# First layer of a two-layer transformer: the token mixer re-ordered, attention values in plain float32

## The chip, the core and the metric

The kernel is one program on one core of a Trainium2 chip. The metric is its time on the device in microseconds (us). A profile of one execution shows the engines of the core: PE (matrix products), PEld (its weight loads), DVE and ACT (element-wise work), POOL and SP (here mostly issuing transfers).

## The reference, cut to what matters

The program computes a first layer (adaptive modulation, a mixer made of windowed attention and a gated convolution, then 16 experts) and a second network of feed-forward blocks and attention. Only the first layer's mixer is touched; `x` has 512 tokens of 1024 channels, `ctx` has 256:

```python
mod = silu(c) @ w_ada + b_ada            # six vectors of 1024; also for c_ctx
hc = modulate(rmsnorm(ctx, g_mix), csh1, csc1)
k_c, v_c = split(hc @ w_in[:, 512:768])
h = modulate(rmsnorm(x, g_mix), sh1, sc1)
q, k, v, bg, cg, hv = split(h @ w_in)    # 512, 128, 128, 512, 512, 512
att = windowed_attention(rope(q), rope(k), v, k_c, v_c, sink)
conv = bg * conv3(cg * hv)
x = x + gt1 * (concatenate([att, conv]) @ w_out)
```

Attention has 8 query heads in two key groups of four heads (group 0 and 1, 64 channels each). A block of 128 queries sees all 256 context keys and the 256 or 384 keys near it.

## The kernel before, in words

Most products are made in three parts (`mm3`, L247 to L249): both operands are split into a high and a low half in the type fp32r (`whi`, `wlo` for weights, by ACT in L161 and DVE in L162), and high x high, low x high and high x low are added up in PSUM. Weights come through a queue object, `W`: chunks of up to 1 MB are loaded by SP into a ring of four buffers, a unit of a chunk is split two units ahead of its use, and a chunk's buffer is free again when it has been split (or, for the raw `w_ada` chunks, multiplied). The order of the chunks is the order of the `plan_...` calls.

The mixer runs in these steps, which follow each other in the program:

- The first third of `w_ada` (8 chunks of 1 MB), multiplied as plain float32 with 32 columns of the array for each of four column groups (L478). While it loads, the six blocks of 128 token rows arrive; ACT and POOL find their norms and DVE scales them.
- Keys and values: for each of the six token blocks PE turns the rows (L294), ACT and DVE apply scale and shift to eight pieces of 128x128 each from PSUM and split the result (L519, L522, L523: `hcT`, `hT`), and 24 products of 256 columns make keys and values (in pA).
- Rotation and turning of the keys (L580), then 96 products of 512 columns for the queries, whose rotation and turning (L605) runs beside the convolution's products: 4 channel blocks x 3 projections x 24 products of 512 columns, in pB and pC by turns.
- Attention: for the eight pairs of query block and key group, `scores` (L687 to L703: products, maximum, exponential, scaling) is called one pair ahead of `values`. There PE turns the probabilities of four heads for one key block (L712, four turns of 128x128 into pB), ACT and DVE split them (`PTh`, `PTl`), and one `mm3` with `Vh`, `Vl` adds to pC; 36 such key blocks in all. `ada_group`, the second and the third part of `w_ada`, runs whole before the second and the fifth pair.
- The output projection: 8 x 4 x 2 `mm3` with `w_out`; when a block of 128 tokens is complete, DVE multiplies it (L786) and adds it to `X`, which POOL has loaded again from `x` (L733).

A scheduler places the instructions on each engine's queue; each engine works its queue off in order. PSUM has two buffers each of pA (two banks), pB and pC.

Of the kernel before, what the change touches and what calls it, by code (L numbers as in the profile page):

```python
# [9 lines left out]
F32 = mybir.dt.float32  # L10
# [180 lines left out]
def tile_net(ctx, tc, I, out):  # L191
# [149 lines left out]
    for c2 in range(2):  # L341
        cs = [W.chunk([(0, P, rows(w_in, 0, K, b0 + c2 * 256, 256))], (P, K, 256)) for b0 in (1280, 1792, 768)]
        for cc in range(2):
            for c in cs:
                W.unit(c, lambda v, cc=cc: v[:, :, cc * P:(cc + 1) * P])
    plan_ada(1)
    plan_ada(2)
# [102 lines left out]
    Vh = mixp.tile([P, 6, P], F32R, name="Vh")  # L450
    Vl = mixp.tile([P, 6, P], F32R, name="Vl")
# [6 lines left out]

    def token_rows(src, t):
        r = early.tile([P, D], F32, name="xrow", tag="xrow", bufs=6)  # L460
        nc.scalar.dma_start(out=r, in_=src[t * P:(t + 1) * P])
        return r
# [4 lines left out]
    def ada_rows(pool, g):  # L467


        bb = pool.tile([P, 512], F32, name="bb", tag="rp1", bufs=1)  # L470
# [3 lines left out]
        p = psB()  # L474
        for k in range(K):
            w = W.next()
            for j in range(4):
                PE.matmul(p[32 * j:32 * j + 32], cb[:, k].rearrange("p s c -> p (s c)"), w[:, j],  # L478
                          start=k == 0, stop=k == K - 1)
        V.tensor_add(bb, p, bb)  # L480
        return bb
# [12 lines left out]
    for r in rows_in:  # L494
        V.tensor_scalar(r, r, row_rstd(early, r, D), None, op0=OP.mult)
    m = ada_rows(early, 0)
# [16 lines left out]
    def modulated_into(pool, dst, t, sc, sh, pick=None):  # L513

        def put(g, m, pv):
            for a in range(m):
                k = g + a
                c_ = slice(t * P, (t + 1) * P)
                A.activation(dst[0][:, k, c_], pv[:, a], AF.Identity, scale=sc[:, k:k + 1], bias=sh[:, k:k + 1])  # L519
            tmp = pool.tile([P, 4, P], F32, name="mtmp", tag="mtmp", bufs=1)  # L520
            for a in range(m):
                V.tensor_scalar(tmp[:, a], pv[:, a], sc[:, g + a:g + a + 1], sh[:, g + a:g + a + 1], op0=OP.mult, op1=OP.add)  # L522
            V.tensor_sub(dst[1][:, g:g + m, c_], tmp, f(dst[0][:, g:g + m, c_]))  # L523
        return put

    hcT = qT.rearrange("p h s -> p (h s)").rearrange("p (s k n) -> p s k n", s=2, k=K)
    hcT = [hcT[:, 0], hcT[:, 1]]
    hT = pair("hT")
# [20 lines left out]
    def turned(b):  # L549
        xs, t, s = (hcT, b, 1) if b < TC else (hT, b - TC, 0)  # L550
        transposed(rows_in[b], K, modulated_into(early, xs, t, sc1[:, s], sh1[:, s]))
        return xs, t

    nxt = turned(0)
    for b in range(6):
        xs, t = nxt
        if b < 5:
            nxt = turned(b + 1)
        o = psA()[:, 0:256]
        for k in range(K):  # L560
            mm3(o, [x[:, k, t * P:(t + 1) * P] for x in xs], [x[:, k % 4] for x in ws[k // 4]], k == 0, k == K - 1)
        A.copy(out=kvs[:, b], in_=o)
    split(Vh, Vl, kvs[:, :, P:256])
    for b0 in (0, 2, 4):
# [11 lines left out]
        for s in range(2):  # L576
            p = psBC()
# [7 lines left out]

    a0, a1 = psA(), psA()
    qp = [a0[:, 0:512], a0[:, 512:1024], a1[:, 0:512], a1[:, 512:1024]]
    for u in range(4):
        w = W.next()
        for kk in range(2):  # L590
            k = u * 2 + kk
            for t in range(T):
                mm3(qp[t], [x[:, k, t * P:(t + 1) * P] for x in hT], [x[:, kk] for x in w], k == 0, k == K - 1)
    qks = []
    for t in range(T):
        qr = rope1(qp[t].rearrange("p (o h d) -> p o h d", o=1, d=HD), 1, H, t, early)
# [4 lines left out]
        for g in range(2):  # L601
            p = psA()
            pv = p[:, :512].rearrange("p (h t) -> p h t", h=4)
# [5 lines left out]
    for cblk in range(4):  # L609
        p3 = []  # L610
        for _ in range(3):
            p3.append(psBC())
            w = W.next()
            for k in range(K):
                mm3(p3[-1], [x[:, k] for x in w], [x[:, k] for x in hT], k == 0, k == K - 1)
        cg = early.tile([P, S], F32, name="cg", tag="rp1", bufs=1)
        A.copy(out=cg, in_=p3[0])
        u_ = early.tile([P, S + 2], F32, name="convu", tag="convu", bufs=1)
        V.memset(u_[:, 0:1], 0.0)
        V.memset(u_[:, S + 1:S + 2], 0.0)  # L620
        V.tensor_mul(u_[:, 1:S + 1], p3[1], cg)
        y = early.tile([P, S], F32, name="convy", tag="rp2", bufs=1)
        V.tensor_scalar(y, u_[:, 0:S], cw[:, cblk, 0:1], None, op0=OP.mult)
        V.scalar_tensor_tensor(y, u_[:, 1:S + 1], cw[:, cblk, 1:2], y, op0=OP.mult, op1=OP.add)
        V.scalar_tensor_tensor(y, u_[:, 2:S + 2], cw[:, cblk, 2:3], y, op0=OP.mult, op1=OP.add)
        V.tensor_mul(conv[:, cblk], p3[2], y)
# [5 lines left out]
    mixT = pair("mixT")  # L632
    for cblk in range(4):
        split(mixT[0][:, 4 + cblk], mixT[1][:, 4 + cblk], conv[:, cblk])
# [9 lines left out]
    def ada_group(g):  # L644
        m = ada_rows(att, g)
# [59 lines left out]

    def values(n, g, Pt, lo, hi):
        o = psC()
        blks = [0, 1] + list(range(2 + lo, 2 + hi))
        for z, blk in enumerate(blks):
# [6 lines left out]
        r = slice(g * 64, g * 64 + 64)  # L716
        ov = o[r].rearrange("p (i t) -> p i t", i=4)
        split(mixT[0][r, 0:4, n * P:(n + 1) * P], mixT[1][r, 0:4, n * P:(n + 1) * P], ov)

    todo = [(n, g) for n in range(T) for g in range(KV)]  # L720
    nxt = scores(*todo[0])
    for z, (n, g) in enumerate(todo):
# [56 lines left out]
    for t in range(T):  # L779
# [3 lines left out]
        for dh in range(2):  # L783
            tmp = att.tile([P, 512], F32, name="tmp", tag=("PTh", "PTl")[dh], bufs=2)
# [678 lines left out]
```

## Time and profile before

| what | us |
|---|---|
| median of three runs (2702.54 to 2704.97) | 2703.97 |
| the profiled execution's own time | 2703.63 |
| its span, first to last instruction | 2701.6 |
| PE busy in the span | 2568.8 |
| last product of the first `w_ada` part begins | 39.05 |
| first product of the convolution begins | 101.83 |
| last product of the convolution begins | 172.44 |
| first finished block of the output projection (L786) | 332.06 |
| first product of the experts (L905) | 388.91 |

Times inside the program count from the start of the span. The profiled execution lies within the runs' range, 0.34 us under their median, so differences worked out in it stand for the runs too.

### The profile page before, as it was taken

The numbers are of one execution on the slowest core, as the hardware profiler recorded it, in microseconds if no ns is written. First come the engines' busy times: TensorE is split into PE (matmuls) and PEld (weight loads), VectorE is DVE, ScalarE is ACT, GpSimd is POOL, SyncE is SP. The second block draws the span as 40 slices with busy tenths as digits, with TensorE's granted clock in tenths as the row PEclk, the third lists the DMA queues.
The fourth block names the chain that finished last, engine by engine and source line by source line (L and its number), as shares of the span: only waits on it lengthen the run. The fifth ranks groups of instructions, "written<-read, shape, count | busy, mean of one in ns | idle before, by whom it ended". The sixth has DMA issues, their size and how long they took to land.

```text
span 2701.6 us, 29081 instructions
## 1 busy us (share of the span) xinstructions
PE 2568.8 (95%) x12042; PEld 1879.9 (70%) x12042; DVE 1066.7 (39%) x1661; ACT 748.4 (28%) x1288; POOL 88.5 (3%) x142
## 2 busy tenths in 40 slices
PE   5988979999998999999999999999999899999999
PEld 3864744333433888878877878887879777878887
DVE  4646441222223433335533334333334566533332
ACT  4324320000002322223322223322223655322221
POOL 1000020000000000000000000000001100000000
PEclk8989979999999999999999999999999999999999
DMA  8226249999998322323222322323232111122321
GB/s 301 67 86 221 71 164 419 414 418 418 416 417 342 124 94 90 105 86 102 74 94 90 106 86 86 108 80 102 78 101 73 63 57 63 63 94 78 108 83 59
DMA packets 179251, 411.89 MB, mean 152 GB/s; under 512 B 7364, under 2 KB 120544, under 8 KB 151472
## 3 DMA queue, kind: packets, MB, share of 16 engines
q1 hardware_dynamic: 176928, 403.73, 40.7%
q0 software_dynamic: 1184, 2.97, 0.4%
q10 hardware_dynamic: 1008, 3.34, 0.3%
q8 instruction: 94, 1.54, 0.2%
q14 instruction: 37, 0.30, 0.0%
HBM read 407.92 MB, written 2.10 MB: 152 GB/s over the span
## 4 chain that ended last, share of the span: by engine, by line
PE 58%; issue 30%; DVE 4%; ACT 3%; DMA 3%; POOL 1%; ACTq 0%; POOLq 0%; DVEq 0%; SPq 0%
PE pA L905 8%; PE pA L247 7%; PE pA L248 7%; PE pA L249 7%; PE pB L905 4%; PE pC L248 2%; PE pC L247 2%; PE pC L249 2%; PE pB L249 2%; PE pB L247 2%; PE pB L248 2%; DMA wraw<-in_w_ada_dram 1%; PE pC L879 1%; PE pC L952 1%; PE ms L1334 1%
## 5 line engine op out<-in xcount | busy, mean ns | idle before, releaser
L161 ACT CAST whi<-wraw 128x1024 fp32r<-128x1024 f32 (+2 forms) x334 | 336.2, 1011 | 1107.6 <-PE pA L248 686.3
L162 DVE TENSOR_TENSOR wlo<-wraw,whi 128x1024 fp32r<-128x1024 f32 (+2 forms) x334 | 392.4, 1177 | 480.1 <-ACT whi L161 472.7
L248 PE MATMUL pA<-xTl,whi 128*128 128x512 f32 (+1 forms) x1536 | 578.7, 377 | 1.6 <-DVE xTl L256 1.6
L249 PE MATMUL pA<-xTh,wlo 128*128 128x512 f32 (+1 forms) x1536 | 578.5, 377 | 0.0
L247 PE MATMUL pA<-xTh,whi 128*128 128x512 f32 (+1 forms) x1536 | 574.7, 382 | 1.5 <-ACT xTh L255 1.3
L247 PEld LDWEIGHTS pA<-xTh,whi 128*128 128x128 f32 x1536 | 290.4, 189 | 76.8 <-ACT sl L989 21.6
L249 PEld LDWEIGHTS pA<-xTh,wlo 128*128 128x128 f32 x1536 | 290.4, 189 | 56.6
L248 PEld LDWEIGHTS pA<-xTl,whi 128*128 128x128 f32 x1536 | 290.8, 189 | 55.2 <-DVE xTl L256 2.1
L991 DVE TENSOR_TENSOR sl<-pA,sl 128x512 f32<-128x512 f32 x88 | 60.9, 692 | 427.3 <-PE pA L249 427.2
L905 PE MATMUL pA<-wraw,wideh 128*64 128x512 f32 x736 | 202.6, 598 | 1.9 <-DMA wraw<-in_w_up_dram 1.4
L249 PE MATMUL pC<-whi,hl 128*128 128x512 f32 x352 | 138.4, 393 | 0.0
L247 PE MATMUL pC<-whi,hh 128*128 128x512 f32 x352 | 138.4, 393 | 0.0
L248 PE MATMUL pC<-wlo,hh 128*128 128x512 f32 x352 | 138.4, 393 | 0.0
L247 PE MATMUL pB<-whi,hh 128*128 128x512 f32 x352 | 138.3, 393 | 0.0
L248 PE MATMUL pB<-wlo,hh 128*128 128x512 f32 x352 | 138.2, 392 | 0.0
L249 PE MATMUL pB<-whi,hl 128*128 128x512 f32 x352 | 138.0, 392 | 0.0
L905 PEld LDWEIGHTS pA<-wraw,wideh 128*64 128x64 f32 x736 | 58.3, 136 | 93.2 <-issue 88.2
L905 PE MATMUL pB<-wraw,hx 128*64 128x512 f32 x344 | 101.0, 597 | 1.1 <-DMA wraw<-in_w_down_dram 1.1
L247 PEld LDWEIGHTS pB<-whi,hh 128*128 128x128 f32 x352 | 66.1, 188 | 15.5 <-DVE X L1040 0.8
L249 PEld LDWEIGHTS pB<-whi,hl 128*128 128x128 f32 x352 | 66.1, 188 | 15.1
L247 PEld LDWEIGHTS pC<-whi,hh 128*128 128x128 f32 x352 | 66.1, 188 | 15.0
L248 PEld LDWEIGHTS pB<-wlo,hh 128*128 128x128 f32 x352 | 66.1, 188 | 14.8
(489 smaller groups left out, 3370.4 us busy)
## 6 DMA issues: line engine op xcount, KB each, us to landing
wraw<-in_w_gate_dram SPq DMA_DIRECT2D x47, 1024.0 KB, 13.3
wraw<-in_w_up_dram SPq DMA_DIRECT2D x45, 1024.0 KB, 12.2
wraw<-in_w_down_dram SPq DMA_DIRECT2D x43, 1024.0 KB, 9.3
wraw<-in_ffn_w_gate_dram SPq DMA_DIRECT2D x40, 1024.0 KB, 5.2
wraw<-in_ffn_w_up_dram SPq DMA_DIRECT2D x40, 1024.0 KB, 5.3
wraw<-in_ffn_w_down_dram SPq DMA_DIRECT2D x32, 1024.0 KB, 4.9
wraw<-in_w_ada_dram SPq DMA_DIRECT2D x24, 1024.0 KB, 9.4
widel<-in_w_up_dram SPq DMA_DIRECT2D x14, 1024.0 KB, 14.0
```

The costliest lines, as they stand in the source:

```text
L161: self.nc.scalar.copy(out=hi, in_=src)
L162: self.nc.vector.tensor_sub(lo, src, f(hi))
L247: PE.matmul(o, a[0], b[0], start=first, stop=False)
L248: PE.matmul(o, a[0], b[1], start=False, stop=False)
L249: PE.matmul(o, a[1], b[0], start=False, stop=last)
L879: PE.matmul(p, ohr[:, t], h[:, t, c_], start=t + z == 0, stop=t + z == T)
L905: PE.matmul(outs[dh][r], x[:, k, r], ws[e][:, j, dh * 512:(dh + 1) * 512], start=k == 0, stop=k == K - 1)
L952: PE.matmul(p, Se[:, t * P:(t + 1) * P], ys[dh][s], start=s == 0, stop=s == 1)
L991: V.tensor_mul(sl, a[:, 512:1024], sl)
L1334: PE.matmul(p[:, :nn], q[a][:, c_], k[b][:, :nn], start=first, stop=False)
```

## The change

The mixer's work is put in another order, and two of its parts are made differently.

- Token rows are turned while the first part of `w_ada` loads (`turned`, between the chunks), back into their own place (`xrows`). Scale and shift are then applied for one block of 128 channels to all tokens at once, from SBUF (`modulated`), and keys and values of all six token blocks are made in step with it, in six accumulators.
- Queries come right behind. The first convolution block runs in three pieces between key and query preparation; the other three run as steps between the pairs of attention, as do the four halves of `ada_group` (`steps`). The order of the weight chunks follows: the convolution's are 0.5 MB each, and six of them stand between the second and third part of `w_ada`. The convolution uses pC alone.
- Probabilities are no longer split: one copy per key block, by ACT and DVE in turn, in float32. Those of group 0 are kept (`stored`), and at group 1 each key block makes two plain float32 products, one per group, each on 64 of the array's 128 columns (e = 0 writes the lower half of pC, e = 1 the upper). The sum goes to `attn` (the upper half of `X`) and is split into `mixT` later (`settle`).

```diff
+    plan_conv(0, 6)
     plan_ada(1)
+    plan_conv(6, 12)
     plan_ada(2)
...
-    m = ada_rows(early, 0)
+    *_, m = ada_rows(early, 0, between=lambda k: turned(k) if k < TC + T else None)
...
+    def modulated(xs, s, k):
+
+        x = xrows[:, :TC] if s else xrows[:, TC:]
+        x, sc, sh = x[:, :, k * P:(k + 1) * P], sc1[:, s, k:k + 1], sh1[:, s, k:k + 1]
+        hi, lo = (v[:, k].rearrange("p (b n) -> p b n", n=P) for v in xs)
+        A.activation(hi, x, AF.Identity, scale=sc, bias=sh)
+        V.tensor_scalar(x, x, sc, sh, op0=OP.mult, op1=OP.add)
+        V.tensor_sub(lo, x, f(hi))
...
-    for b in range(6):
-        xs, t = nxt
-        if b < 5:
-            nxt = turned(b + 1)
-        o = psA()[:, 0:256]
-        for k in range(K):
+    for k in range(K):
+        modulated(hcT, 1, k)
+        modulated(hT, 0, k)
+        for b, o in enumerate(kvp):
+            xs, t = (hcT, b) if b < TC else (hT, b - TC)
             mm3(o, [x[:, k, t * P:(t + 1) * P] for x in xs], [x[:, k % 4] for x in ws[k // 4]], k == 0, k == K - 1)
...
     def values(n, g, Pt, lo, hi):
-        o = psC()
...
+        if g == 0:
+            stored[:] = [att.tile([P, 5, 512], F32, name="PT0", tag="PT0", bufs=1)]
+        else:
+            o = psC()
         for z, blk in enumerate(blks):
             p = psB()
             for i in range(4):
                 PE.transpose(p[:, i * P:(i + 1) * P], Pt[:, i, z * P:(z + 1) * P], ident)
-            PT = [att.tile([P, 512], F32R, name=nm, tag=nm, bufs=2) for nm in ("PTh", "PTl")]
-            split(PT[0], PT[1], p)
-            mm3(o, [Vh[:, blk], Vl[:, blk]], PT, z == 0, z == len(blks) - 1)
...
+            pt = att.tile([P, 512], F32, name="PTl", tag="PTl", bufs=2) if g else stored[0][:, z]
+            (V.tensor_copy if z % 2 else A.copy)(out=pt, in_=p)
+            if g:
+                for e, x in enumerate((stored[0][:, z], pt)):
+                    r = slice(e * 64, e * 64 + 64)
+                    PE.matmul(o[r], Vf[:, blk, r], x, start=z == 0, stop=z == len(blks) - 1)
+        if g:
+            A.copy(out=attn[:, :, n * P:(n + 1) * P], in_=o.rearrange("p (i t) -> p i t", i=4))
...
+    def steps():
...
+        ada1, ada2 = ada_group(1), ada_group(2)
+        c1, c2, c3 = (conv_block(att, c) for c in (1, 2, 3))
+        some(c1, 3)
+        yield
+        some(ada1, 1)
+        yield
+        some(ada1, 1)
+        some(c2, 1)
+        yield
+        some(c2, 2)
+        yield
+        some(c3, 2)
+        yield
+        some(c3, 2)
+        some(ada2, 1)
+        yield
+        some(ada2, 1)
+        yield
...
     for z, (n, g) in enumerate(todo):
         cur = nxt
-        if z in (1, 4):
-            ada_group(1 if z == 1 else 2)
         if z + 1 < len(todo):
             nxt = scores(*todo[z + 1])
         values(n, g, *cur)
+        next(beside, None)
+        if z == 6:
+            mixT = pair("mixT")
+            for cblk in range(4):
+                split(mixT[0][:, 4 + cblk], mixT[1][:, 4 + cblk], conv[:, cblk])
+            for b in range(T - 1):
+                settle(b)
+    settle(T - 1)
```

Three places in the engines' queues show it. First DVE at the start of keys and values, right behind the scale and shift vectors (`sc`, `sh`); `mtmp` and `xrows` hold modulated values, `qT` and `hTl` the low halves of context and latent tokens. Before:

```order
L504 COPY sh_104<-pC 128x8
L162 TENSOR_TENSOR wlo<-wraw,whi 128x1024 x2
L522 TENSOR_SCALAR mtmp<-pB,sc_103,sh_104 128x128 x3
L162 TENSOR_TENSOR wlo<-wraw,whi 128x1024 x2
L522 TENSOR_SCALAR mtmp<-pB,sc_103,sh_104 128x128
L523 TENSOR_TENSOR qT<-mtmp,qT 128x4x128
L522 TENSOR_SCALAR mtmp<-pC,sc_103,sh_104 128x128 x4
L523 TENSOR_TENSOR qT<-mtmp,qT 128x4x128
```

And of the change:

```order
L523 COPY sh_104<-pC 128x8
L538 TENSOR_SCALAR xrows<-xrows,sc_103,sh_104 128x4x128
L539 TENSOR_TENSOR hTl<-xrows,hTh 128x512
L162 TENSOR_TENSOR wlo<-wraw,whi 128x1024 x2
L538 TENSOR_SCALAR xrows<-xrows,sc_103,sh_104 128x2x128 x2
L539 TENSOR_TENSOR qT<-xrows,qT 128x256 x2
L162 TENSOR_TENSOR wlo<-wraw,whi 128x1024 x2
L538 TENSOR_SCALAR xrows<-xrows,sc_103,sh_104 128x4x128
L538 TENSOR_SCALAR xrows<-xrows,sc_103,sh_104 128x2x128
L539 TENSOR_TENSOR hTl<-xrows,hTh 128x512
L539 TENSOR_TENSOR qT<-xrows,qT 128x256
```

The 48 modulations of 128 columns out of PSUM have become eight of 512 and eight of 256 columns out of SBUF, with eight subtractions of each size.

Second, PE in attention at the second query block's group 1. Before (L712 turns probabilities, L247 to L249 are the value products):

```order
L712 MATMUL pB<-cst,Pt 128x128 x8
L247 MATMUL pC<-PTh,Vh 128x512
L248 MATMUL pC<-PTl,Vh 128x512
L249 MATMUL pC<-PTh,Vl 128x512
L247 MATMUL pC<-PTh,Vh 128x512
L712 MATMUL pB<-cst,Pt 128x128
L248 MATMUL pC<-PTl,Vh 128x512
L249 MATMUL pC<-PTh,Vl 128x512
```

And of the change (L735 turns, L741 are the plain products, from `PT_1333`, which is `stored`, for group 0 and `PTl` for group 1; L247 from `hTh` is the third convolution block):

```order
L735 MATMUL pB<-cst,Pt 128x128 x4
L741 MATMUL pC<-PT_1333,Vf 64x512
L741 MATMUL pC<-PTl,Vf 64x512
L735 MATMUL pB<-cst,Pt 128x128 x4
L741 MATMUL pC<-PT_1333,Vf 64x512
L735 MATMUL pB<-cst,Pt 128x128 x4
L741 MATMUL pC<-PTl,Vf 64x512
L741 MATMUL pC<-PT_1333,Vf 64x512
L741 MATMUL pC<-PTl,Vf 64x512
L735 MATMUL pB<-cst,Pt 128x128 x4
L741 MATMUL pC<-PT_1333,Vf 64x512
L735 MATMUL pB<-cst,Pt 128x128 x4
```

Three products have become two, and a product of one half does not always stand next to one of the other: the 36 of them stand in 21 runs, cut by turns of 128 columns.

Third, POOL's queue at the start, where `X` is `x` loaded again for the residual sum (`sinkb` and `cw` are small constants, `ms` and `rstd` the rows' norms). Before:

```order
L508 DMA sinkb<-in_sink_dram 128x8
L511 DMA cw<-in_conv_w_dram 128x4x1 x3
L733 DMA X<-in_x_dram 128x1024 x2
L262 ISA
L262 TENSOR_SCALAR ms<-ss 128x1 x3
L263 TENSOR_TENSOR rstd<-ms,mhalf 128x1 x3
```

And of the change:

```order
L527 DMA sinkb<-in_sink_dram 128x8
L530 DMA cw<-in_conv_w_dram 128x4x1 x3
L262 ISA
L262 TENSOR_SCALAR ms<-ss 128x1
L263 TENSOR_TENSOR rstd<-ms,mhalf 128x1
```

Two of the four loads of `X`, 0.5 MB each, have left the start; all four now stand behind the loads for both `ada_group`s. From the middle of the output projection on, every engine has the same instructions in the same order as before.

## Rows read from the trace of the kernel before

**Rows 1.** Timeline at the start: start us, duration, engine, line, operation, idle time before.

```profile
10.47 0.54 POOL L733 DMA_DIRECT2D X<-in_x_dram  x1 [0.67 <-DVE ccol L491]
...
39.05 1.94 PE L478 MATMUL pB<-wraw,cb 128*32 128x512 f32 x8 [1.51 <-DMA wraw<-in_w_ada_dram]
...
43.17 0.16 DVE L504 COPY sh<-pC 128x8 f32<-128x8 f32 x1
```

**Rows 2.** Busy time by stage: engine us (instructions), granted clock, share of DMA, GB/s.

```profile
core 0: us, PE busy (x) PEld busy (x) DVE busy (x) ACT busy (x) POOL busy (x), PEclk, DMA share, GB/s
14.00:41.00 27.00, 14.16 (x68) 2.25 (x68) 4.52 (x6) 4.60 (x8) 4.64 (x10) 0.96 1.02 403
41.00:56.00 15.00, 9.74 (x44) 9.21 (x45) 11.85 (x24) 9.48 (x20) 0.61 (x1) 0.62 1.05 356
56.00:80.00 24.00, 22.02 (x165) 20.07 (x164) 21.19 (x56) 16.31 (x47) 0.00 (x0) 1.00 0.02 7
...
173.00:200.00 27.00, 19.79 (x99) 13.52 (x100) 16.74 (x40) 12.26 (x28) 1.12 (x2) 0.75 0.18 56
200.00:216.00 16.00, 12.16 (x83) 5.75 (x77) 8.59 (x23) 4.35 (x11) 0.09 (x1) 1.00 1.01 422
216.00:245.00 29.00, 26.45 (x161) 20.14 (x160) 22.10 (x46) 15.37 (x35) 1.91 (x4) 1.00 0.14 51
245.00:270.00 25.00, 19.11 (x110) 8.22 (x109) 11.50 (x27) 9.42 (x18) 0.00 (x0) 0.86 0.92 312
270.00:300.00 30.00, 25.34 (x141) 19.42 (x141) 21.78 (x46) 15.62 (x36) 0.00 (x0) 1.00 0.30 91
```

**Rows 3.** Groups of DVE's instructions by line, 41 to 83 us: busy us, mean ns.

```profile
L522 DVE TENSOR_SCALAR mtmp<-pB,sc,sh 128x128 f32<-128x128 f32 x24 | 8.3, 404 | 0.7 <-DVE qT L523 0.5
L162 DVE TENSOR_TENSOR wlo<-wraw,whi 128x1024 fp32r<-128x1024 f32 x5 | 5.9, 1222 | 1.9 <-ACT whi L161 1.9
L523 DVE TENSOR_TENSOR hTl<-mtmp,hTh 128x512 fp32r<-128x512 f32 x8 | 5.5, 688 | 0.1
L542 DVE TENSOR_TENSOR rp<-rp,rp 128x256 f32<-128x256 f32 x2 | 0.8, 416 | 0.0
```

**Rows 4.** Groups by line with shapes apart, 0 to 420 us: same columns.

```profile
L703 DVE TENSOR_SCALAR Pt<-Pt,sm 128x640 f32<-128x640 f32 x16 | 7.8, 550 | 0.1
L703 DVE TENSOR_SCALAR Pt<-Pt,sm 128x512 f32<-128x512 f32 x16 | 6.7, 482 | 0.1
```

**Rows 5.** Timeline: convolution's first and last products, first block of the output projection.

```profile
101.83 0.39 PE L247 MATMUL pB<-hTh,whi 128*128 128x512 f32 x1
102.07 0.40 PE L248 MATMUL pB<-hTl,whi 128*128 128x512 f32 x1
...
172.44 0.40 PE L249 MATMUL pC<-hTh,wlo 128*128 128x512 f32 x1
...
332.06 1.29 DVE L786 TENSOR_TENSOR tmp<-pA,gt 128x512 f32<-128x512 f32 x2 [7.30 <-PE pA L249]
```

**Rows 6.** Timeline: turns of probabilities on PE, and the raw `w_ada` products between others.

```profile
195.75 0.50 PE L247 MATMUL pC<-PTh,Vh 128*128 128x512 f32 x1
196.18 1.92 PE L478 MATMUL pB<-wraw,cb 128*32 128x512 f32 x16
198.03 0.50 PE L248 MATMUL pC<-PTl,Vh 128*128 128x512 f32 x1
198.37 0.40 PE L249 MATMUL pC<-PTh,Vl 128*128 128x512 f32 x1
...
223.60 1.04 PE L712 MATMUL pB<-cst,Pt 128*128 128x128 f32 x8
```

**Rows 7.** Chain of waits in the experts: start us, length, engine, line.

```profile
388.91 27.69 PE pA L905 x128
```

**Rows 8.** Timeline in the experts: plain float32 products on halves of the columns.

```profile
400.55 0.59 PE L905 MATMUL pA<-wraw,wideh 128*64 128x512 f32 x1
400.56 0.59 PE L905 MATMUL pA<-wideh 128*64 128x512 f32 x1
```

**Rows 9.** Who waited for whom, 173 to 300 us: us, times, longest us.

```profile
PE pA L687 <- ACT Pt L696: 10.9, 10, 5.6
...
PE pB L478 <- DMA wraw<-in_w_ada_dram: 5.0, 4, 2.7
```

More of the change, by code (lines that the diff above doesn't have):

```diff
@@ L340, in tile_net, with plan_conv @@
     plan_cols(w_in, K, 0, 512, 4, 2)
[L341 to L345, printed above, removed]
+    def plan_conv(u0, u1):
+        for u in range(u0, u1):
+            b0 = (1280, 1792, 768)[u % 3] + u // 3 * P
+            c = W.chunk([(0, P, rows(w_in, 0, K, b0, P))], (P, K, P))
+            W.unit(c, lambda v: v)
+    plan_conv(0, 6)
     plan_ada(1)
+    plan_conv(6, 12)
     plan_ada(2)
@@ L473, in ada_rows @@
             nc.gpsimd.dma_start(out=bb[32 * j:32 * j + 32], in_=b_ada[:, c0:c0 + 512].to_broadcast([32, 512]))
-        p = psB()
-        for k in range(K):
[L476 to L481, printed above, removed]
+        for k0 in (0, 4):
+            p = psB() if g else psA()[:, 0:512]
+            for k in range(k0, k0 + 4):
+                w = W.next()
+                for j in range(4):
+                    PE.matmul(p[32 * j:32 * j + 32], cb[:, k].rearrange("p s c -> p (s c)"), w[:, j],
+                              start=k == k0, stop=k == k0 + 3)
+                if between is not None:
+                    between(k)
+            V.tensor_add(bb, p, bb)
+            yield bb
     def spread(dst, rows_, j):
@@ L493, in tile_net, with turned, put @@
         V.tensor_copy(cb[:, :, s], ccol[:, s, :, None].to_broadcast([P, K, 16]))
-    for r in rows_in:
+    hcT = qT.rearrange("p h s -> p (h s)").rearrange("p (s k n) -> p s k n", s=2, k=K)
+    hcT = [hcT[:, 0], hcT[:, 1]]
+    hT = pair("hT")
+    def turned(b):
+        r = rows_in[b]
         V.tensor_scalar(r, r, row_rstd(early, r, D), None, op0=OP.mult)
-    m = ada_rows(early, 0)
+        def put(g, m, pv):
+            (A.copy if g else V.tensor_copy)(out=r[:, g * P:(g + m) * P].rearrange("p (a n) -> p a n", n=P), in_=pv)
+        transposed(r, K, put)
+    *_, m = ada_rows(early, 0, between=lambda k: turned(k) if k < TC + T else None)
     pc = psC()
@@ L563, in tile_net @@
[L563 removed]
+    a0 = psA()
+    kvp = [a0[:, 0:256], a0[:, 512:768], psB()[:, 0:256], psB()[:, 0:256], psC()[:, 0:256], psC()[:, 0:256]]
+    for k in range(K):
[3 more added lines that the diff above has]
+            xs, t = (hcT, b) if b < TC else (hT, b - TC)
+            mm3(o, [x[:, k, t * P:(t + 1) * P] for x in xs], [x[:, k % 4] for x in ws[k // 4]], k == 0, k == K - 1)
+    for b, o in enumerate(kvp):
+        (V.tensor_copy if b % 2 else A.copy)(out=kvs[:, b], in_=o)
@@ L564, in tile_net @@
+    first = conv_block(early, 0)
+    next(first)
+    A.copy(out=Vf, in_=kvs[:, :, P:256])
     for b0 in (0, 2, 4):
@@ L583, in tile_net @@
                                              in_=p.rearrange("p (g t) -> p g t", g=KV))
[L586 to L594, printed above, removed]
     for t in range(T):
+        if t % 2 == 0:
+            next(first)
         qr = rope1(qp[t].rearrange("p (o h d) -> p o h d", o=1, d=HD), 1, H, t, early)
@@ L631, in tile_net @@
     att = st.enter_context(tc.tile_pool(name="att", reuse_waits=RW, bufs=2))
-    mixT = pair("mixT")
-    for cblk in range(4):
-        split(mixT[0][:, 4 + cblk], mixT[1][:, 4 + cblk], conv[:, cblk])
+    attn = Xf[:, 4 * S:8 * S].rearrange("p (c s) -> p c s", s=S)
     gf = att.tile([4, 256], F32, name="gf", bufs=1)
@@ L644, in ada_group @@
     def ada_group(g):
-        m = ada_rows(att, g)
+        halves = ada_rows(att, g)
+        next(halves)
+        yield
+        m = next(halves)
         p = psB()
```

98 lines of the change are left out of this document (47 added, 51 removed).

## The prediction

> **What bounds the kernel now.** I read the timeline of the start first, then busy time by stage, DVE's groups, and who waited for whom.
>
> The start is bound by transfers: from 14 to 41 us the queues move 403 GB/s [rows 2], and the last `w_ada` product begins at 39.05 when its chunk lands [rows 1]. Keys and values are bound by DVE: it is busy for 11.85 of 15 us and then 21.19 of 24 [rows 2], mostly with 48 modulations of 128 columns (two groups of 24) and twelve subtractions of 512 (eight are shown) [rows 3]; PE's clock is 0.62 of full in the first of the two stretches. From 101.83 to 172.44 the convolution runs with PE without a gap, a product each 0.235 us (0.24 between the first two starts) [rows 5]. Attention is where PE waits: in the five stretches from 173 to 300 it is idle for 7.2, 3.8, 2.6, 5.9 and 4.7 us, 24.2 in all [rows 2]. Besides, the first ran at a clock of 0.75 and the fourth at 0.86, which costs about 0.25 x 19.8 + 0.14 x 19.1 = 7.6 us. So 31.8 us could come back there. The waits named are scores for the exponentials that free their banks, 10.9 us, and raw products for `w_ada` transfers, 5.0 us [rows 9].
>
> I take the first finished block of the output projection, at 332.06 [rows 5], as the mark. Behind it nothing changes in any engine's order, so what the mark gains, the kernel gains.
>
> **The change, to the last query product.** Two loads of `X`, 1.05 MB, leave the start (one is shown [rows 1]). At 403 GB/s they took 2.6 us. Turning rows there adds 48 PE turns and 12 copies, hidden by the waits for transfers: PE is busy for 14.2 of 27 us [rows 2]. They would cost only if a late row held up a chunk; rows arrive before the chunk they stand ahead of. So the last product ends at 39.05 + 1.94 - 2.6 = 38.4, and the scale and shift vectors are there 2.3 us later as now (43.33 against 40.99 [rows 1]): 40.7.
>
> DVE then has eight rounds of four instructions: a scaling of 512 columns at 0.482 us, one of 256 at 0.346 (the 68 ns for 128 columns between the two forms [rows 4], carried down to 256), a subtraction of 512 at 0.688 and one of 256 at 0.416 [rows 3]. That is 1.93 us a round, 15.5 in all; with five weight splits of 1.222 it is 21.6, until 62.3. Before, the same part took 48 x 0.344 (8.3 us for 24, overlaps taken off) + 12 x 0.688 + the splits. PE's own share, 18 products of 256 columns a round, is about 18 x 0.118 = 2.1 us at full clock, so PE keeps nearly level with DVE and ends 0.5 us later, at 62.8. In the queue eight of the 96 query products stand before that; the other 88 take 20.7 us, to 83.5. Before, this point is 101.83. Gain: 18.3 us. If PE's clock stays at half and DVE is held by it, up to 5 us of this go; if DVE's instructions overlap by 0.08 us as its modulations do (0.404 long, 0.344 apart), 2 us are added.
>
> **From there to the mark.** PE's work in plain products: the value products before are 36 x 3 x 0.235 = 25.4 us. For the new ones the experts have the same form: one gate and up step issues 64 plain products (two trace entries each), 27.69 us [rows 7], or 0.433 a product, with the two halves' entries starting 0.01 us apart [rows 8]; a pair costs 0.865 and, since two of one half cannot overlap, so does a single one. In the order the 36 stand in 21 runs; counting one slot of 0.865 for each two that alternate, and one for each left over, gives 27 slots, 23.4 us. All pairs whole would be 18 slots, 15.6; none, 36 slots, 31.1. I take 23.4, since the order says it: a gain of 2.0. The 24 turns of keys now lie behind this point, 24 x 0.13 = 3.1 us more (1.04 us for eight [rows 6]). The copies in place of splits take one of ACT and DVE off the way of each key block; neither is the bound, so this is counted only in the waits below.
>
> Switching between the full array and column tiles costs something: from a full product to a set on 32 columns 0.43 us passed instead of 0.235, and on the way back the next full product came after 0.34 [rows 6]. That is 0.3 for a way in and out; 21 runs make 6.3 us. Before, the turns between the value products cost part of that too; I take a net 4. The Trainium skill, TensorEngine Tiling (Array Packing), section Key Properties, says that changing the tiling mode drains TensorE, and that speaks against putting such products singly between turns. With a drain that shows a product's whole tail, 0.59 - 0.433 = 0.16 us, at all 42 switches, the term would be 6.7 and the total 3 us higher than by the rows.
>
> What waits stay? Chains of softmax, copies and products: in the best stretch PE idles 2.6 of 29 us [rows 2]; with 144 convolution products more to put between, 8 us over a stretch of some 115. Key and query turning wait for DVE and ACT, whose queues have weight splits standing ahead of them that need a buffer from the first convolution projection: 5 us. The two `ada_group`s load four chunks ahead and four after: 4 MB at 422 GB/s [rows 2] is 10 us, which begin when the first half is multiplied and have the next pair's scores, turns and values beside them: 1.5 us each, 3 together. With the 4 for switching: 20 of 31.8 us remain, 11.8 come back. Nothing coming back, and more lost, is the next part's rival; all of it but the switching is the other bound, 27.8.
>
> Smaller convolution chunks are twice as many and half as large; one feeds 24 products, 5.6 us, and takes 1.2 us at 422 GB/s, so they are hidden. The four loads of `X` now start late, two of them when the last pair is settled; the projection's products still ahead take 138 x 0.235 = 32 us, so these are hidden too.
>
> Sum: 18.3 + 2.0 - 3.1 + 11.8 = 29.0 us off. The profiled execution took 2703.6, the runs' median 2704.0; I predict **2675**.
>
> **Rivals.**
> - *Only the front gains.* Attention loses elsewhere what the filling wins: in-order queues let a late exponential hold up convolution products that could run. For it: ACT and DVE have 73% and more of some stretches to do (21.8 of 30 us on DVE [rows 2]). Then 18.3 + 2.0 - 3.1 = 17 off, less up to 4 for switching: 2687 to 2691.
> - *The packing doesn't pack.* All 36 run singly: 31.1 in place of 23.4, so 7.7 worse than my sum: 2682. For it are the single products in the order; against it are the experts' pairs.
> - *The holes fill.* 27.8 back in place of 11.8, and with pairs whole 7.8 more: 2651 to 2659. Against it: even the best stretch idles.
> - *Slower.* DVE and ACT hold the splits of convolution weights in order. Behind `ada_group` four of them stand ahead of the next pair's maxima; they wait for chunks that load only when raw chunks have been multiplied. If such a stop hits each of the eight pairs, PE's extra wait must exceed 29 + 20 = 49 us in all, 6 a pair, to end slower than before. The waits for `w_ada` now are 2.7 us at the longest [rows 9], so only a chain of several would do it.
>
> **Chances.** My sum, 2668 to 2682, 0.50; front alone or no packing, 2682 to 2695, 0.24; holes filled, below 2668, 0.18; no change 0.03; slower 0.05. A change under 0.2%, 5.4 us, can't be told from none. So faster 0.92, same 0.03, slower 0.05. The range, 2656 to 2692, leaves out the slower case and the ends of the others.
>
> **What would show it.** After: last raw product of the first part near 38; the first convolution product near 83.5, with DVE over 85% busy before 62; value products 0.43 apart in pairs and 0.865 singly; the mark near 303; the experts' first product 29 us before 388.9. The prediction is wrong if the mark gains much less than the queries do, that is, if PE idles for more than 30 us between them, or if `w_ada` still ends at 41.

## The result, and the profile after

The changed kernel takes 2660.83 us (median of four runs, 2660.04 to 2662.10) where the kernel before takes 2703.26 (2702.13 to 2704.97, the earlier three and one more): a ratio of 0.9843, 95% interval 0.9826 to 0.9860, or 42.4 us less. The forecast was 2675, 29.0 us less, with a range from 2656 to 2692. The sign and the range held; the gain was half as large again as the sum, and below it is shown where. The two profiled executions are 43.1 us apart (2703.63 and 2660.51).

Timeline of the change, single rows from several stretches (start us, duration, engine, line, operation): the last raw `w_ada` product of the first part, the last query product and the first one of the convolution, the first finished block of the output projection, the experts' first product.

```profile
37.01 1.06 PE L483 MATMUL pA<-wraw,cb 128*32 128x512 f32 x8 [0.35 <-DMA wraw<-in_w_ada_dram]
...
83.69 0.39 PE L249 MATMUL pA<-whi,hTl 128*128 128x512 f32 x1
83.92 0.39 PE L247 MATMUL pC<-hTh,whi 128*128 128x512 f32 x1
...
293.06 0.69 DVE L849 TENSOR_TENSOR tmp<-pA,gt 128x512 f32<-128x512 f32 x1 [7.30 <-PE pA L249]
...
349.78 1.51 PE L968 MATMUL pA<-wraw,wideh 128*64 128x512 f32 x6 [0.49 <-DVE wideh L951]
```

Against [rows 1, 5, 7]: the raw products end 2.9 us earlier (38.1, was 41.0), the first convolution product comes 17.9 earlier, the mark 39.0, the experts 39.1. So in these two executions 17.9 us were gained up to the last query product, and 21.1 between there and the mark (the first finished block of the output projection).

Busy time by stage of the change (columns as in [rows 2]):

```profile
14.00:38.00 24.00, 18.79 (x112) 7.95 (x112) 9.02 (x14) 8.44 (x16) 4.14 (x10) 1.00 1.01 389
41.00:63.00 22.00, 19.90 (x146) 19.35 (x147) 19.44 (x38) 14.29 (x22) 0.62 (x1) 0.92 0.50 160
...
84.00:133.00 49.00, 47.65 (x264) 38.77 (x262) 35.73 (x83) 19.89 (x42) 2.00 (x4) 1.00 0.23 79
133.00:180.00 47.00, 43.62 (x244) 22.10 (x242) 31.27 (x69) 21.96 (x46) 1.96 (x4) 1.00 0.67 224
180.00:230.00 50.00, 50.00 (x237) 33.90 (x236) 21.42 (x47) 13.09 (x29) 0.00 (x0) 1.00 0.08 27
230.00:263.00 33.00, 29.56 (x169) 14.37 (x168) 19.38 (x38) 14.26 (x27) 1.12 (x2) 0.95 0.94 309
```

PE idles for 1.4, 3.4, 0 and 3.4 us in the last four stretches shown, 8.2 in all, where five stretches of attention had 24.2 before; the clock is below full in one of them only. Two waits that answer to [rows 9], 84 to 293 us, have become short:

```profile
PE pA L703 <- ACT Pt L712: 3.8, 4, 1.4
PE pB L483 <- DMA wraw<-in_w_ada_dram: 2.6, 2, 1.9
```

DVE's groups from 36 to 70 us, beside [rows 3, 4]: the durations behind the front's sum.

```profile
L539 DVE TENSOR_TENSOR hTl<-xrows,hTh 128x512 fp32r<-128x512 f32 x8 | 5.5, 682 | 0.0
L538 DVE TENSOR_SCALAR xrows<-xrows,sc,sh 128x512 f32<-128x512 f32 x8 | 4.3, 538 | 0.7 <-ACT hTh L537 0.7
L539 DVE TENSOR_TENSOR qT<-xrows,qT 128x256 fp32r<-128x256 f32 x8 | 3.2, 415 | 0.0
L538 DVE TENSOR_SCALAR xrows<-xrows,sc,sh 128x256 f32<-128x256 f32 x8 | 3.2, 405 | 0.0
```

The value products of the change, in two places of the timeline: a run of three with the pair in front, and one where the product of group 0 (from `PT`) goes first.

```profile
139.54 0.64 PE L741 MATMUL pC<-PTl,Vf 128*64 128x512 f32 x1
139.54 0.64 PE L741 MATMUL pC<-PT,Vf 128*64 128x512 f32 x1
140.02 0.59 PE L741 MATMUL pC<-PTl,Vf 128*64 128x512 f32 x1
140.03 0.59 PE L741 MATMUL pC<-PT,Vf 128*64 128x512 f32 x1
140.45 1.02 PE L741 MATMUL pC<-PTl,Vf 128*64 128x512 f32 x2
141.40 0.66 PE L735 MATMUL pB<-cst,Pt 128*128 128x128 f32 x4
...
173.69 1.07 PE L741 MATMUL pC<-PT,Vf 128*64 128x512 f32 x2
173.79 0.59 ACT L737 COPY PTl<-pB 128x512 f32<-128x512 f32 x1
174.43 1.07 PE L741 MATMUL pC<-PTl,Vf 128*64 128x512 f32 x2
175.44 0.66 PE L735 MATMUL pB<-cst,Pt 128*128 128x128 f32 x4
```

In the first place two products start in the same instant and take 0.9 us together. In the second, the product of group 0 needs nothing but a kept copy and starts at once; its partner waits for the copy that ACT ends at 174.38, and by then the first is nearly through: 1.75 us for the two. Of 18 pairs only 6 overlap in the change. Eleven products stand alone (1.00 to 1.06 us each up to the next operation, one wait left out), five runs of three take 1.86, one pair 1.01, four pairs in the wrong order 1.75 to 1.85: 28.6 us in all. One that stands alone, with four turns behind it, and the weight loads (PEld) of both:

```profile
141.99 1.07 PE L741 MATMUL pC<-PT,Vf 128*64 128x512 f32 x2
142.99 0.66 PE L735 MATMUL pB<-cst,Pt 128*128 128x128 f32 x4
143.57 0.64 PE L741 MATMUL pC<-PTl,Vf 128*64 128x512 f32 x1
...
141.98 0.19 PEld L741 LDWEIGHTS pC<-PT,Vf 128*64 128x64 f32 x2 [0.17 <-issue]
142.99 0.42 PEld L735 LDWEIGHTS pB<-cst,Pt 128*128 128x128 f32 x4 [0.81 <-issue]
```

### The profile page after: what moved, and what is told of

Read it like the earlier page. It is cut to its first block, busy times and chain, and to the rows that moved or that the text cites. A ratio compares the mean times of both kernels' runs of the same rounds, so it can differ in the third digit from the quotient of the medians.

```text
span 2658.6 us, 28917 instructions
## 1 busy us (share of the span) xinstructions
PE 2552.4 (96%) x12006; PEld 1856.7 (70%) x12006; DVE 1045.2 (39%) x1620; ACT 735.8 (28%) x1243; POOL 88.2 (3%) x142
## 4 chain that ended last, share of the span: by engine, by line
PE 60%; issue 30%; DMA 3%; DVE 3%; ACT 3%; POOL 1%; SPq 0%; POOLq 0%; ACTq 0%; DVEq 0%
PE pA L968 9%; PE pA L247 7%; PE pA L248 7%; PE pA L249 7%; PE pB L968 4%; PE pC L249 3%; PE pC L248 3%; PE pC L247 3%; PE pB L248 2%; PE pB L249 2%; PE pB L247 2%; PE pC L942 1%; PE ms L1397 1%; PE pC L1015 1%; PE pC L741 1%
## 5 line engine op out<-in xcount | busy, mean ns | idle before, releaser
L249 PE MATMUL pA<-xTh,wlo 128*128 128x512 f32 (+1 forms) x1536 | 578.2, 377 | 0.0
L247 PE MATMUL pA<-xTh,whi 128*128 128x512 f32 (+1 forms) x1536 | 574.0, 381 | 1.5 <-ACT xTh L255 1.3
L247 PEld LDWEIGHTS pA<-xTh,whi 128*128 128x128 f32 x1536 | 289.8, 189 | 76.8 <-ACT sl L1052 21.7
L249 PEld LDWEIGHTS pA<-xTh,wlo 128*128 128x128 f32 x1536 | 289.9, 189 | 56.6
L247 PE MATMUL pC<-whi,hh 128*128 128x512 f32 x352 | 138.4, 393 | 0.0
L249 PE MATMUL pC<-whi,hl 128*128 128x512 f32 x352 | 138.4, 393 | 0.0
L247 PE MATMUL pB<-whi,hh 128*128 128x512 f32 x352 | 138.2, 393 | 0.0
L249 PE MATMUL pB<-whi,hl 128*128 128x512 f32 x352 | 138.1, 392 | 0.0
L247 PEld LDWEIGHTS pB<-whi,hh 128*128 128x128 f32 x352 | 66.1, 188 | 15.5 <-DVE X L1103 0.7
L249 PEld LDWEIGHTS pB<-whi,hl 128*128 128x128 f32 x352 | 66.1, 188 | 14.9
L247 PEld LDWEIGHTS pC<-whi,hh 128*128 128x128 f32 x352 | 66.1, 188 | 14.9
```

Source lines behind the costliest of these rows:

```text
L247: PE.matmul(o, a[0], b[0], start=first, stop=False)
L249: PE.matmul(o, a[1], b[0], start=False, stop=last)
```

## The experiments

Each kernel ran beside the kernel before on the same chip (its median there was 2703.0 to 2704.8), four to six times. "Mark" is the first finished block of the output projection in the one profiled execution, 332.1 before and 293.1 after. "Stretch" is the time from the first convolution product to the mark there, 230.2 before. Two medians can't be told apart below some 4 to 5 us, by the intervals; mark and stretch leave out what happens later, but are from one execution each.

| kernel | median us | ratio to before, 95% | mark | stretch |
|---|---|---|---|---|
| the change | 2660.8 | 0.9843 (0.9826 to 0.9860) | 293.1 | 209.1 |
| split_values | 2683.3 | 0.9924 (0.9911 to 0.9936) | 312.3 | 228.7 |
| whole_steps | 2671.7 | 0.9878 (0.9863 to 0.9893) | 302.2 | 216.9 |
| front_only | 2685.0 | 0.9930 (0.9917 to 0.9942) | 316.5 | 232.9 |
| rev | 2652.1 | 0.9812 (0.9798 to 0.9826) | 284.8 | 200.4 |
| split_conv_first | 2661.3 | 0.9843 (0.9828 to 0.9858) | 291.8 | 208.0 |
| claim | 2680.5 | 0.9916 (0.9899 to 0.9932) | 312.8 | 227.3 |
| load | 2664.8 | 0.9858 (0.9843 to 0.9872) | 294.8 | 211.6 |
| early_x | 2662.4 | 0.9847 (0.9833 to 0.9862) | 295.0 | 209.4 |
| rev_spread | 2648.4 | 0.9795 (0.9778 to 0.9812) | 279.7 | 194.6 |
| whole_chain | 2672.3 | 0.9884 (0.9865 to 0.9903) | 305.8 | 222.2 |
| whole_claim | 2670.6 | 0.9877 (0.9860 to 0.9894) | 299.9 | 217.1 |
| whole_single | 2681.0 | 0.9917 (0.9905 to 0.9930) | 311.9 | 228.2 |

The start is not the same from one execution to the next. The change and all of these but early_x have the same instructions in the same order there; in their twelve traces the last raw product ends between 38.0 and 40.1 us, and the first convolution product begins between 82.8 and 85.5. So a difference of two marks stands for the runs to some 2 us only; the stretch leaves the start out.

**The parts, undone one by one.** First the values, back in three products:

```diff
+        o = psC()
...
-            pt = att.tile([P, 512], F32, name="PTl", tag="PTl", bufs=2) if g else stored[0][:, z]
-            (V.tensor_copy if z % 2 else A.copy)(out=pt, in_=p)
...
+            split(PT[0], PT[1], p)
+            mm3(o, [Vh[:, blk], Vl[:, blk]], PT, z == 0, z == len(blks) - 1)
+        r = slice(g * 64, g * 64 + 64)
+        A.copy(out=attn[r, :, n * P:(n + 1) * P], in_=o[r].rearrange("p (i t) -> p i t", i=4))
```

> The changed kernel with one part undone: each key block's probabilities are split again and multiplied by the value halves in three products on the whole array, group by group. Theory A (the filled waits and the early keys and queries are the gain, the half-array products are worth nothing to PE): in the trace of the change the 21 runs of half-array products take 28.6 us from their first start to the next operation, and three products take 36 x 3 x 0.235 = 25.4; so PE's own work falls by about 3 us, while ACT and DVE get one more operation of 0.6 us per key block, 36 in all, of which a third may show: 2655 to 2668, near the change's 2660.8. Theory B (the packed products save PE time, as the prediction's sum had it, or more): 2 us without the waits, and up to 10 with them, slower: 2663 to 2673. A rival C, in which the lighter chain of copies is what removed the waits of attention: PE idles again for some 20 us and the time is 2680 or more.

22.4 us slower: by time rival C, and neither A nor B. Next the interleaving, with the values packed:

```diff
-    plan_conv(0, 6)
+    plan_conv(0, 12)
     plan_ada(1)
-    plan_conv(6, 12)
     plan_ada(2)
...
+    for c in (1, 2, 3):
+        for _ in conv_block(att, c):
+            pass
...
+        if z in (1, 4):
+            for _ in ada_group(1 if z == 1 else 2):
+                pass
...
-        next(beside, None)
```

> The changed kernel with the other three convolution blocks put whole ahead of attention, and both parts of the modulation weights whole before the second and the fifth pair, with the weight chunks in that order; packed values and the early keys and queries stay. Theory A (the interleaving fills PE's waits): the 16 us of idle PE and the 6 us of slow clock that the change took out come back: 2680 to 2684. Theory C (the copies in place of splits shorten the chain, and the waits went with them): less than 8 us come back: 2661 to 2669.

10.9 slower, between the two. And both undone:

> The changed kernel with both undone: split values in three products, and convolution and modulation weights whole; left of the change is the front (rows turned while the first modulation weights load, scale and shift for all tokens at once, six accumulators) and the turning of keys and queries beside the first convolution block. Theory A: 18.3 us earlier at the last query product, less 3.1 for turns of keys moved behind it, gives 15 off: 2688, and the last query product still ends at 83.9. Theory C, in which the front is worth more since its clock is better and attention starts with a fuller queue: under 2682. If the front gives nothing in the end (its gain waits for weights later): 2700.

2685.0, 18.5 less than before and 3 under theory A, and a mark 15.6 us ahead of the kernel before, where 18.3 - 3.1 = 15.2 was the term: the front is about as large as forecast. But the parts don't add. With the steps whole, packing is worth 13.3; with them interleaved, 22.4. Interleaving is worth 10.9 with packed values and 1.8 with split ones. By the stretches the four are 16.0, 19.6, 7.8 and 4.2: the same direction, but 3.6 us where the medians have 9.1, so how far they fail to add is not settled. What holds the block back in the interleaved order shows in the trace of split_values; first two stretches of its busy time, then rows of PE's timeline in the second.

```profile
84.00:107.00 23.00, 21.11 (x108) 16.59 (x106) 17.28 (x36) 8.55 (x18) 0.00 (x0) 1.00 0.43 149
107.00:133.00 26.00, 14.43 (x65) 12.17 (x66) 14.79 (x38) 9.33 (x21) 2.00 (x4) 0.54 0.03 11
```

```profile
107.42 1.06 PE L640 MATMUL pB<-cst,qk 128*128 128x128 f32 x8 [1.91 <-DVE qk L636]
111.65 1.97 PE L640 MATMUL pB<-cst,qk 128*128 128x128 f32 x8 [3.17 <-DVE qk L636]
...
121.73 0.58 PE L704 MATMUL pA<-kTh,qT 128*128 128x256 f32 x1 [2.75 <-ACT Pt L713]
...
133.22 0.48 PE L247 MATMUL pC<-PTh,Vh 128*128 128x512 f32 x1
133.53 0.39 PE L247 MATMUL pC<-hTh,whi 128*128 128x512 f32 x1
```

For 26 us PE has only scores and turns, of queries and at the end of probabilities, most of them behind DVE or ACT; it idles 11.6 us and its clock falls to 0.54. The second convolution block, which fills this stretch in the change, begins at 133.53, right behind the first value product. The value accumulator `o` is taken from the two buffers of pC when `values` is called, and the block's step is called after that: the block stands behind the claim. In the change, group 0 takes no accumulator, so nothing stands ahead of the block. That is a fourth theory, D. Two kernels test it from both sides. One gives split_values its block back:

```diff
+        if z == 0:
+            next(beside, None)
         values(n, g, *cur)
-        next(beside, None)
+        if z:
+            next(beside, None)
```

> The run with split values, and the first step beside attention (the whole second convolution block) called before the values of the first pair instead of after them. Where the values come first in the program, their accumulator takes a buffer of pC ahead of the block, and on PE's queue the block stands behind the first value product: PE was half idle from 107 to 133 us at a clock of 0.5. Theory D (who claims pC first is what made 22 us between split and packed values): with the block ahead PE's hole closes, 9 us of idle and some 8 of slow clock come back: 2662 to 2669, so that packing itself is worth no more than 2 to 8. Theory C (a lighter chain of copies is what helps): the hole is made good later by other waits, 2676 to 2683.

22.0 us came back: 2661.3 against the change's 2660.8, so less is left for packing than the 2 to 8 us of the expectation. The same two stretches, and the second one in the change:

```profile
84.00:107.00 23.00, 23.00 (x118) 18.59 (x117) 17.02 (x36) 8.77 (x18) 0.00 (x0) 1.00 0.44 153
107.00:133.00 26.00, 24.30 (x140) 19.98 (x139) 19.27 (x49) 11.29 (x25) 2.00 (x4) 1.00 0.03 11
...
107.00:133.00 26.00, 24.65 (x147) 20.23 (x145) 18.90 (x49) 11.08 (x24) 2.00 (x4) 1.00 0.03 11
```

The other leaves the packed values and takes an accumulator at group 0 as well:

```diff
             stored[:] = [att.tile([P, 5, 512], F32, name="PT0", tag="PT0", bufs=1)]
+            o = psC()
...
+            if not g and z in (0, len(blks) - 1):
+                PE.transpose(o[:, 0:P], Pt[:, 0, z * P:(z + 1) * P], ident)
```

> The changed kernel with an accumulator of pC taken at group 0 too, before the next step beside attention is called; two turns of 128 columns per group 0 write it and nothing reads it. The products and copies of the change stay. Theory D: the second convolution block falls behind the first pair's turns and the hole opens in this kernel too, 15 to 18 us and 1 us for eight turns: 2674 to 2680. Theory C: only the turns show, 2661 to 2664.

19.7 slower, with the same hole:

```profile
107.00:133.00 26.00, 12.96 (x59) 10.77 (x59) 15.63 (x39) 8.66 (x18) 2.00 (x4) 0.58 0.03 11
```

Theory D holds in the interleaved order: the packed products themselves are worth 0.5 us there, which can't be told from nothing (the stretch is even 1.1 shorter with split values), and what they do for the time is that they claim their buffer late. The load that they take off DVE was tried by itself:

```diff
+            junk = att.tile([P, 416], F32, name="junk2", tag="junk2", bufs=1)
+            V.tensor_sub(junk, pt[:, :416], pt[:, 96:512])
```

> The changed kernel with one more DVE subtraction of 416 columns per key block, 36 of some 0.57 us, whose result nobody reads: the load of a split's second operation without its place in the chain. Theory C (DVE's load is what packing relieved): 20 us more on DVE while maxima and copies wait behind it, 5 to 15 us slower, 2666 to 2676. Theory D: PE's queue has convolution products to go on with, 0 to 4 us slower, 2661 to 2665.

3.9 slower, 1.7 at the mark, 2.5 in the stretch: inside theory D's bounds, and hardly more than a measurement can tell.

**The order of the two products.**

```diff
-                for e, x in enumerate((stored[0][:, z], pt)):
+                for e, x in ((1, pt), (0, stored[0][:, z])):
```

> The changed kernel with the two half-array products of a key block issued in the other order: first that of group 1, which needs the copy just made, then that of group 0, whose copy is kept. On PE's queue all 36 then stand alternately, in 10 runs of one to two pairs instead of 21 mixed ones. Theory A (in the change the products run singly because the one that is ready goes first and the other waits 0.55 to 0.66 us for its copy; pairs whose two are ready start together): 18 slots of 0.865 us and some 0.25 for each way in and out, 18.5 us in place of 28.6 to 31: 8 to 11 us faster than the change, 2650 to 2653. Theory B (the copy's wait only moves ahead of the pair, where PE then stands still 18 times for up to 0.6 us): 0 to 3 us faster, 2658 to 2661. If two half-array products can't overlap next to 128x128 turns at all: 2661.

8.8 us faster than the change, 8.3 at the mark, 8.7 in the stretch: theory A. All 18 pairs overlap, in 12 runs of 17.3 us together. (Counted again, the change has 30 slots, not 29.) Its timeline, two key blocks:

```profile
173.81 0.64 PE L741 MATMUL pC<-PTl,Vf 128*64 128x512 f32 x1 [0.24 <-ACT PTl L737]
173.82 0.64 PE L741 MATMUL pC<-PT,Vf 128*64 128x512 f32 x1
174.29 0.59 PE L741 MATMUL pC<-PTl,Vf 128*64 128x512 f32 x1
174.30 0.59 PE L741 MATMUL pC<-PT,Vf 128*64 128x512 f32 x1
174.72 0.59 PE L741 MATMUL pC<-PTl,Vf 128*64 128x512 f32 x1
174.73 0.59 PE L741 MATMUL pC<-PT,Vf 128*64 128x512 f32 x1
175.15 0.59 PE L741 MATMUL pC<-PTl,Vf 128*64 128x512 f32 x1
175.16 0.59 PE L741 MATMUL pC<-PT,Vf 128*64 128x512 f32 x1
175.68 1.09 PE L735 MATMUL pB<-cst,Pt 128*128 128x128 f32 x8
```

Four products in 1.87 us, where the change takes 1.86 for three. PE waits 0.24 for the copy: the product that must wait goes first, and the one that is ready goes with it.

**The transfers at the start.** The two early loads of `X` again, unused:

```diff
+    for t in (2, 3):
+        nc.gpsimd.dma_start(out=X[:, t], in_=x_in[t * P:(t + 1) * P])
```

> The changed kernel with the two early loads of X put back behind the small constants on POOL's queue, 1.05 MB that nothing uses. The prediction's step: the start is bound by transfers, 1.05 MB at 403 GB/s delay the last modulation chunk by 2.6 us, 2663.4. A rival: the chunks' rows are held by the turning of token rows between them, and a late row costs more, 4 to 6 us. Or the loads fill gaps in the queues: no change, 2660.8.

The raw products end at 40.0 instead of 38.1, and the mark is 1.9 later, the median 1.6. The direction is the prediction's, but claim, which has none of these loads, ends the same products at 40.1 (first its last row of them, then that of early_x):

```profile
39.08 1.06 PE L483 MATMUL pA<-wraw,cb 128*32 128x512 f32 x8 [0.67 <-DMA wraw<-in_w_ada_dram]
```

```profile
37.88 2.13 PE L483 MATMUL pA<-wraw,cb 128*32 128x512 f32 x16
```

Besides, in early_x the turns of token rows stand elsewhere among the raw products than in the change. So the price of the two loads is not shown: 2.6 us and nothing both fit, and nothing speaks for 4 to 6.

**A faster version.** What is left in rev are waits for the second halves of `w_ada`; one convolution projection goes between the halves, in the steps and in the plan of chunks:

```diff
+    plan_ada(1, 0, 4)
+    plan_conv(6, 7)
+    plan_ada(1, 4, 8)
+    plan_conv(7, 11)
+    plan_ada(2, 0, 4)
+    plan_conv(11, 12)
+    plan_ada(2, 4, 8)
```

> The run with the products in the other order, and one projection of a convolution block between the two halves of each part of the modulation weights, in the steps and in the order of the weight chunks, so that PE has 24 products to do while the second half loads. In the trace of that run PE waits 3.4 us for those chunks, 1.6 for their sum, and has a clock of 0.71 from 240 to 250 us, 3 us. If the load is what PE waits for: 4 to 8 us faster than that run's 2652.1, 2644 to 2648. A rival: the smaller chunk between the raw ones takes one of four buffers and the second half's chunks start no earlier, so that the wait only moves: 2650 to 2654.

2648.4, 3.7 less than rev and just above what was expected; the medians are too near to be told apart, the marks are 5.1 apart and the stretches 5.8. By its median it is the fastest kernel of this study.

**What stays open: packing with the steps whole.** There packing is worth 13.3 us, though no block waits behind the claim. Three kernels looked for the reason: a chain as long as a split's,

```diff
-            (V.tensor_copy if z % 2 else A.copy)(out=pt, in_=p)
+            A.copy(out=pt, in_=p)
+            V.tensor_scalar(pt, pt, 1.0, None, op0=OP.mult)
```

> The run with the steps whole (2671.7), and each key block's copy made in two operations one behind the other, ACT's copy and DVE's multiplication by 1.0 in place, as long a chain as a split has. Theory C for an attention with nothing put between (there split values took 13 us more): chain and load are what the packing relieved, and 8 to 14 us come back, 2680 to 2686. Theory D (the accumulator that group 0 claims, or the three products themselves): 0 to 4, 2671 to 2676.

the claim of the experiment above,

> The run with the steps whole (2671.7), with an accumulator of pC taken at group 0 and written by two turns of 128 columns, read by nobody. Theory D, that the claim costs wherever values stand ahead of other work: 8 us or more, 2680 and up. Theory C: there is no convolution block behind the claim to hold back, so only eight turns show, 1 us, 2671 to 2674.

and lone plain products, group by group, with nothing kept:

```diff
+            pt = att.tile([P, 512], F32, name="PTl", tag="PTl", bufs=2)
+            (V.tensor_copy if z % 2 else A.copy)(out=pt, in_=p)
+            PE.matmul(o[r], Vf[:, blk, r], pt, start=z == 0, stop=z == len(blks) - 1)
```

> The run with the steps whole (2671.7), with values again group by group: one copy per key block as there, and behind it at once one plain float32 product on 64 columns, into an accumulator of its own; nothing is kept from group 0. PE then issues 36 lone products of 0.865 us in place of 29 slots, 6 us more, and each waits for the copy of its own key block. Theory E (in an attention with nothing put between, the kept copies of group 0 are work that waits for nothing, half of all products, and that is where 13 us went): 2681 to 2692. Theory F (the three products and two splits in fp32r are what cost 13 us there, whatever is kept): only the 6 us show, 2674 to 2679.

The claim costs nothing. Chain and load cost 0.6 us by the medians, 3.6 at the mark and 5.3 in the stretch, in an execution 4.9 us slower than its median: not the whole reason, though a part of it can't be excluded. The lone products cost 9.2: at the lower edge of theory E, 2 us above the other's range, and within the measurement's width of both. The trace leans to theory F. From 160 us on PE idles for 12.9 us in whole_steps up to the mark, 15.2 in whole_single up to 310, and 20.3 in front_only up to the mark:

```profile
160.00:302.20 142.20, 129.29 (x690) 75.40 (x689) 71.83 (x161) 52.07 (x112) 4.22 (x8) 0.98 0.46 165
```

```profile
160.00:310.00 150.00, 134.80 (x673) 74.26 (x673) 71.87 (x160) 54.37 (x116) 4.22 (x8) 0.97 0.45 156
```

```profile
160.00:316.50 156.50, 136.22 (x717) 92.12 (x716) 83.75 (x180) 61.77 (x132) 4.21 (x8) 0.93 0.43 150
```

So without kept copies PE waits some 2 us more, and most of the 9.2 is its own time; with split values it waits 7 us more, at a lower clock. What in the splits and their three products brings those waits stays open.

## Why the prediction came out as it did

- **The start** (2.6 us): its size is not shown. The last product ends at 38.1, forecast 38.4, but at up to 40.1 in other executions of the same start; against the one of before, 41.0, that is 0.9 to 3.0 us, and early_x can't be told from this spread.
- **Keys, values, queries** (18.3, the start included): right, 17.9 (16.4 to 19.1 over the twelve traces). DVE is busy for 19.44 of the 22 us from 41 to 63, 88%. The four instructions take 0.538, 0.405, 0.682 and 0.415 us, where 0.482, 0.346, 0.688 and 0.416 were taken from before; the two scalings are longer, and they overlap. The first convolution product was forecast for 83.5 and came at 83.92.
- **Value products** (2.0 less, with a net 4 for switching): near in sum, with both parts mis-sized. By the prediction's own rule the order gives 26 slots, not 27; the trace has 30, because the rule took each two that alternate for a pair, and in four runs the second waits for its copy. The switching term was right before the net: a lone product keeps PE for 1.00 us and not 0.865, and four turns behind one take 0.58 and not 0.4, so 0.3 a way in and out. But the three products have ways of their own. Counted from each start to the next, waits left out, they take 29.6 us in split_conv_first, not 25.4, against 28.6 for the half-array products; the turns of probabilities take 15.4 there and 17.9 in the change. That is 1.5 us more for the change in all, and PE's busy time from the last query product to the mark, at full clock, is alike (201.0 x 0.99 = 199.0, and 199.9 at 1.00, less 0.9 that lie before). So the net loss is 0 to 1.5 us, where 4 - 2.0 = 2.0 was forecast.
- **Key turns behind the point** (3.1): near. 24 turns at 0.79 us for eight in the change are 2.4.
- **Waits** (20 of 31.8 us stay): this is the step that failed. "Key and query turning wait for DVE and ACT ... 5 us": PE idles 1.4 from 84 to 133. "Chains of softmax, copies and products ... 8 us over a stretch of some 115": nothing from 180 to 230, and 3.4 from 133 to 180. The `ada_group`s are near, 2.6 against 3. Over the whole way to the mark, waits and slow clock fell from 24.2 + 8.2 to 8.2 + 2.0: 22 us came back, not 11.8 (15.8 without the 4 for switching). The rate of the best stretch of before was carried over to a stretch with other work between, which does not idle at such a rate.
- **Why the waits went** the prediction had only in half. It saw the steps between the pairs; it didn't see that they run early only because group 0 takes no accumulator ahead of them. split_values and claim show that, 22 and 20 us. The rival "only the front gains" (2687 to 2691), convolution products held in order behind a late exponential, is in its mechanism what happens with the same steps and split values: 2683, 4 us below it. (Of its reason, 73% and more of some stretches, only DVE's share is so; ACT had 15.62 of those 30 us, 52%.)
- **Rivals.** "The packing doesn't pack" is true of 12 pairs in 18: 30 slots for 27 are 2.6 us by its price, not 7.7, and the packing done whole (rev) gains 8.8 more. "The holes fill" is the nearest: 22 of its 27.8 us, without the pairs. "Slower" is out. The time fell below 2668, a class with a chance of 0.18; the class of the sum had 0.50. The range held because it was 36 us wide, not because the term for the waits was right.
- **Behind the mark** no gain was claimed, and the profiled executions differ by 4.0 us there. From mark to end they take 2369.5 us before and 2365.5 after, and 2363.8 to 2370.8 in the twelve experiments, with no order in it. From 2300 to 2340 us the kernel before ran at a clock of 0.91, the same part of the program in the change at 1.00 (first the row of before, then that of the change); 0.09 of its 36 busy us are 3.2 us.

```profile
2300.00:2340.00 40.00, 35.95 (x211) 30.80 (x211) 23.97 (x38) 15.82 (x30) 4.56 (x8) 0.91 0.17 54
```

```profile
2260.00:2300.00 40.00, 36.23 (x236) 31.36 (x236) 23.01 (x35) 14.90 (x29) 4.55 (x8) 1.00 0.17 53
```

So some 39 of the 42.4 us belong to the change, and the rest can't be told from the spread of executions.

## What to carry to other kernels

When work is put between other work, look at which of the two takes the shared buffers first: an accumulator taken a step too early held back a whole convolution block, 20 us, with no product longer than before. Two products on halves of the array run together only if both can start, so issue first the one that must wait. And where two parts of a change are worth more together than apart, undo each with the other in place, and look for what ties them.

## What the runs showed of the hardware

- A lone half-array product delays what follows: the next full weight load starts only 0.81 us after the end of the one before it, and a product of 0.865 us (two entries 0.43 apart in a pair) keeps PE for 1.00; the four turns behind it take 0.58 and not 0.4. The Trainium skill, TensorEngine Tiling (Array Packing), section Key Properties, says that a change of tiling mode drains TensorE; the trace fits this, with about 0.3 us for a way in and out.
- Two products on different halves of the columns ran together when both were ready as the first was issued: all 18 pairs in rev (1.01 us for a pair by itself), and 6 of 18 in the change, where a pair whose second waited took 1.75 to 1.85 us.
- PE's clock followed its waits within one stretch: half idle from 107 to 133 us, split_values ran at 0.54 of full, most of the time at the lower of its two levels (1.2 of 2.4 GHz); with a convolution block between the same turns and scores, split_conv_first ran at 1.00.
